# Meta split and row squares put in program order on ScalarE and VectorE, in a hybrid attention layer

## The chip, the core and the metric

The kernel runs on one core of one Trainium2 chip. The time is the device time of one execution in microseconds; lower is better. Each kernel is run several times and the median counts. The engines are named as in the profile: PE is TensorE's matmul, PEld its weight load, DVE VectorE, ACT ScalarE, POOL GpSimd and SP SyncE, whose queue issues nearly all DMAs.

## The reference

One decoder layer over 2048 tokens of width 1024, with 16 learned meta tokens in front. Two kinds of attention run side by side: stick-breaking attention with 8 heads, and a sliding window of 128 with 16 query heads, 2 key heads and a sink per head. Gates merge the two branches, and an RMSNorm ends the layer. Cut to what matters here:

```python
xn = rms_norm(h, norm_gain[l])          # x * rsqrt(mean(x * x) + eps) * gain
proj = xn @ w_in[l]
sb_q, sb_k, sb_v, sw_q, sw_k, sw_v, sb_z, sw_z, g_sb, g_sw = jnp.split(proj, offsets, axis=-1)
# stick-breaking, for each block of 128 queries
mask = (s[None, :] < t[:, None]) & valid[None, :end]
log_beta = jax.nn.log_sigmoid(z)
log_1m = jnp.where(mask, log_beta - z, 0.0)
rev = lax.cumsum(log_1m, axis=3, reverse=True)
suffix = jnp.concatenate([rev[..., 1:], jnp.zeros_like(rev[..., :1])], axis=-1)
w = jnp.where(mask, jnp.exp(log_beta + suffix), 0.0)
o = w @ v
# after both branches
merged = jax.nn.sigmoid(g_sb) * y_sb + jax.nn.sigmoid(g_sw) * y_sw
h = h + merged @ w_out[l]
return rms_norm(h, final_norm_gain)[:, BLOCK:]
```

## The kernel before

The sequence is reversed, so that a running product along a row goes from the newest key to the oldest and ends at the 16 meta columns. The tokens form four groups of 512, handled in two halves: groups 2 and 3 first, then 0 and 1. Each float32 operand of a product is split into a rounded part and the remainder (h and l), and a product is three matmuls: h by h, h by l, l by h.

Each half runs the projections and the window attention (`window`), then the stick-breaking attention (`stick`) with gate projections (`gemm`, L464) woven between its steps. The first half ends with eight pairs of gates that share products (`gate_pairs`); the second goes on to the branch and output projections (`finish`).

The order of work has two sources. PE's instructions run in the order of the program text in the whole kernel. ACT, DVE and SP follow the text only in some stretches (`tc.manual_schedule`). Elsewhere, in `stick` and in `gate_pairs` from its first `ordered()` on, a planner simulates the program when it is built and gives each engine, whenever that is free, the instruction that is then ready and stands first in the text. Each engine then works through its list strictly in order, waiting on the chip wherever an input is late. So an instruction whose inputs are ready early in the simulation is put ahead of work that stands before it in the text.

`stick` walks over steps (h, g, n, j): head, query group, key group counted from the query's, and block of 128 queries.

- `row` makes one row of a step: matmuls into one or two "z" banks (L918), a sigmoid into a row buffer (ACT, L921), in the second half a triangle set to one on POOL (L923), and the running product along the row (DVE, L926 or L928). Where the row ends at the meta columns, POOL copies its last 16 columns to `mr` (L934).
- `turn`, six steps later in the first half and five in the second, transposes four blocks of rows (L943) and splits them with `evac_split`: the copy L126 on ACT, the remainder L127 on DVE.
- `values` multiplies the turned blocks with the values (L975); the last one of a (h, g) copies the sum out (L981) and stores it.
- `split_meta`, called once per (h, g) behind the turn with i = 0 of the last key group, splits `mr` into `m`: the copy L953 on ACT and the remainder L954 on DVE. One turn later, behind the transposes of i = 1, `turn_meta` transposes `m` on PE (L959) and copies the four quarters to `wm` (L963), which a later `values` reads. With 8 heads and 2 groups in each half there are 32 such splits.

`sums_ahead` prepares the norms of the second half's tokens while `gate_pairs` runs. It is advanced once per pair (`next(along, None)`), behind the sigmoid of the pair's first gate (`gate_out`, L1138 or L1141). In each of the first four pairs it loads four tiles of x (128 by 512, into a ring of four buffers, `xs`) and squares them on ACT with a running sum (L1107). With the fifth it makes the reciprocal root (L1112, then `rsqrt`, L131 to L140, with a logarithm and an exponential on ACT). The last pair calls `prep`, which uses the result. A pair's weights are split at L115 and L119, combined at L1078 to L1087, and the combinations split at L1092 and L1094; L1133 adds a product's bank to other sums on DVE and so frees the bank.

Of the kernel before, what the change touches and what calls it, by code (L numbers as in the profile page):

```python
# [10 lines left out]
AF = mybir.ActivationFunctionType  # L11
ALU = mybir.AluOpType
# [31 lines left out]
def f32(ap):  # L44
    return ap.bitcast(F32)
# [3 lines left out]
def tile_kernel(ctx, tc, x, xt, meta, metat, gain, w_in, w_sb, w_sw, w_out, sinks, fgain,  # L49
# [6 lines left out]
    V, A, G, T = nc.vector, nc.scalar, nc.gpsimd, nc.tensor  # L56

    def DMA(dst, src):
        nc.sync.dma_start(*(t.bitcast(F32) if t.dtype == F32R else t for t in (dst, src)))
# [69 lines left out]
    def rsqrt(r, ssq, pool, mid=lambda: None, t=None):  # L129

        V.tensor_scalar(ssq, ssq, 1.0 / D, EPS, op0=ALU.mult, op1=ALU.add)  # L131
        A.activation(r, ssq, AF.Ln)
        A.activation(r, r, AF.Exp, scale=-0.5)
        mid()
        if t is None:
            t = pool.tile([P, 4], F32, tag="nwt", name="nwt", bufs=2)[:r.shape[0], :r.shape[1]]
        V.tensor_tensor(t, r, r, op=ALU.mult)
        V.tensor_tensor(t, t, ssq, op=ALU.mult)
        V.tensor_scalar(t, t, -0.5, 1.5, op0=ALU.mult, op1=ALU.add)
        V.tensor_tensor(r, r, t, op=ALU.mult)  # L140
# [252 lines left out]
    def ring_x(dt=F32):  # L393
        return tp.tile([P, GT], dt, tag="xs", name="xs", bufs=XS)

    def sums():
        return tp.tile([P, 2, 4], F32, tag="ssq", name="ssq", bufs=3)
# [455 lines left out]
    def stick(groups, bp):  # L853
# [96 lines left out]
        def split_meta(h, g):  # L950
            st = state[h, g]
            m = st["m"] = bp.tile([P, 4, 2, NM], F32R, tag="m", name="m", bufs=2)
            A.copy(m[:, :, 0], st["mr"])  # L953
            V.tensor_tensor(m[:, :, 1], st["mr"], f32(m[:, :, 0]), op=ALU.subtract)  # L954

        def turn_meta(h, g):
            p, a = divmod(h, 2)
# [31 lines left out]
        for s in range(n + lt + 3):  # L989
            if s < n:  # L990
                row(*steps[s])
                yield 0.45 if s >= lt else 1.31
            t = s - lt
            if 0 <= t < n:
                turn(*steps[t])
                turned.append(s)
                yield 0.43
                h, g, step, i = steps[t]
                if g + step == 3 and i == 0:
                    split_meta(h, g)  # L1000
                if g + step == 3 and i == 1:
                    turn_meta(h, g)
                    yield 0.11
                if g + step == i == 3:
                    av_todo.append((h, g, vm[:, h // 2, h % 2, :], wm[g % 2], None, False, True))
                    turned.append(s)
            while av_todo and turned[0] < s - 1:
                del turned[0]
                yield values()
# [89 lines left out]
    def sums_ahead(gs_, rs, short):  # L1099

        ssqs = [sums() for _ in gs_]
        todo = [(g, ssq, i, f) for g, ssq in zip(gs_, ssqs) for i in range(4) for f in range(2)]
        while todo:
            for g, ssq, i, f in todo[:4]:
                t = ring_x()
                DMA(t, x[g * GT + i * P:g * GT + (i + 1) * P, f * GT:(f + 1) * GT])
                A.activation(t, t, AF.Square, accum_out=ssq[:, f, i:i + 1])  # L1107
            del todo[:4]
            yield
        t, u = (short()[:, :8] for _ in range(2))  # L1110
        for n, ssq in enumerate(ssqs):
            V.tensor_tensor(t[:, 4 * n:4 * n + 4], ssq[:, 0], ssq[:, 1], op=ALU.add)  # L1112
        rsqrt(rs, t, tp, t=u)
# [237 lines left out]
    for half, groups in enumerate(halves):  # L1351
        gts = [lambda spec=spec: gate(*spec) for spec in specs[half]]
        with tc.tile_pool(name=f"swa{half}", bufs=1, side="left") as sp:
            m = half == 0
# [70 lines left out]
        if half == 0:  # L1425
            with tc.tile_pool(name="fast", bufs=1, side="left") as bp:
                pairs = list(zip(specs[0][-FAST::2], specs[0][-FAST + 1::2]))
                sums_x = combined(*groups, bp, short, *early)
                byhand = ExitStack()
                byhand.enter_context(tc.manual_schedule(engines={mybir.EngineType.DVE}))  # L1430
                with tc.manual_schedule(engines={mybir.EngineType.Activation}):
                    for n in range(PLAIN):
                        w, use, _ = plain[n]
                        for g in groups:
                            next(sums_x[4])
                            if n + 1 == PLAIN and g == groups[1]:
                                drain(first_pair)
                            drain(lagged(col_tile(w, g, use)))
                        if n + 2 < PLAIN:
                            plain.append(gts[rest + n + 2]())  # L1440
                        elif n + 2 == PLAIN:
                            nxt = []
                            first_pair = pair_weights(pairs[0][0][0], pairs[0][1][0], bp, nxt, True)
                            next(first_pair)
                    drain(sums_x[4])
                    sums_x[5]()
                rs = tp.tile([P, 8], F32, tag="rs8", name="rs", bufs=1)
                rs0, rs1 = rs[:, :4], rs[:, 4:]
                gate_pairs(*groups, pairs, bp, sums_x, nxt, byhand.close, sums_ahead(halves[1], rs, short),
                           lambda: prep(halves[1][0], rs0))  # L1450
                hsplit[0] = False
# [68 lines left out]
```

## Time and profile before

| | us |
|---|---|
| median of 3 runs | 2091.56 |
| lowest, highest | 2090.66, 2092.18 |
| profiled execution | 2093.26 |
| its span, first to last instruction | 2091.4 |

The profile is of one execution. Its page gives the busy time of each engine, the span in 40 slices, and the costliest groups of instructions. A timeline row has the start and the duration in us, the engine, the line, the operation, what it writes and reads, and the shape; "x3" stands for three in a row, and the bracket at the end tells how long the engine stood idle before it and what ended that. A row of a tile or a line has the shortest, median and longest duration in ns and the first and last start. Busy times in 40 slices of 52 us each:

```profile
PE   9999999999999999999999999999999999999998
PEld 7888888888888888888888888888888888788887
DVE  7897986877687754887728788777774547464543
ACT  6677774577665335777735555655653212321121
POOL 1233444331000000233310000000000343000000
PEclk9999999999999999999999999999999999999999
```

The first half's stick stage takes slices 8 to 11 (about 360 to 560 us), the gate pairs slices 12 to 15 (about 590 to 745 us), the second half's stick stage slices 22 to 31 (about 1100 to 1590 us). The granted clock is full throughout.

### The profile page before, as it was taken

How to read it: one execution, taken by the hardware profiler on the slowest of the kernel's cores; microseconds unless marked ns; L12 is line 12 of the kernel's file. 1: busy time of each engine (PE TensorE's matmuls, PEld its weight loads, DVE VectorE, ACT ScalarE, POOL GpSimd, SP SyncE). 2: the span in 40 equal slices, each digit the busy share in tenths (PEclk: the TensorE clock that was granted, in tenths of full speed). 3: DMA queues.
4: the chain of work that ended last, by engine and by line, in shares of the span. 5: the costliest groups of instructions: out<-in, count | busy, mean ns of one | idle time of the engine just before them, and what ended most of it. 6: DMA issues, size and time to landing. Idle time of an engine off the chain costs nothing. (4 is left out here: it accounts for less than half of the span.)

```text
span 2091.4 us, 30949 instructions
## 1 busy us (share of the span) xinstructions
PE 2076.3 (99%) x10579; PEld 1744.8 (83%) x10579; DVE 1463.0 (70%) x2383; ACT 1091.4 (52%) x2657; POOL 345.7 (17%) x682
## 2 busy tenths in 40 slices
PE   9999999999999999999999999999999999999998
PEld 7888888888888888888888888888888888788887
DVE  7897986877687754887728788777774547464543
ACT  6677774577665335777735555655653212321121
POOL 1233444331000000233310000000000343000000
PEclk9999999999999999999999999999999999999999
DMA  9855555866377574435455344343424987568532
GB/s 338 307 195 201 188 175 179 252 199 185 91 278 298 209 247 163 159 126 177 150 171 161 120 130 129 114 129 98 121 83 165 350 318 223 182 229 305 154 100 91
DMA packets 170093, 391.46 MB, mean 187 GB/s; under 512 B 23728, under 2 KB 28208, under 8 KB 169936
## 3 DMA queue, kind: packets, MB, share of 16 engines
q1 hardware_dynamic: 169648, 389.23, 55.8%
q8 instruction: 83, 1.36, 0.3%
q14 instruction: 74, 0.61, 0.1%
q10 hardware_dynamic: 288, 0.27, 0.0%
HBM read 241.68 MB, written 145.18 MB: 185 GB/s over the span
## 5 line engine op out<-in xcount | busy, mean ns | idle before, releaser
L464 PE MATMUL ps_g<-xh,wh 128*128 128x512 f32 x1264 | 517.0, 409 | 1.1 <-DVE tmp L680 0.6
L464 PE MATMUL ps_g<-xl,wh 128*128 128x512 f32 x1264 | 495.6, 392 | 0.7 <-DVE xl L1199 0.6
L464 PE MATMUL ps_g<-xh,wl 128*128 128x512 f32 x1264 | 495.7, 392 | 0.0
L928 DVE TENSOR_TENSOR_SCAN row<-row 128x512 f32<-128x512 f32 (+4 forms) x256 | 290.1, 1134 | 116.2 <-POOL row L923 60.1
L464 PEld LDWEIGHTS ps_g<-xh,wl 128*128 128x128 f32 x1264 | 237.8, 188 | 52.7
L464 PEld LDWEIGHTS ps_g<-xh,wh 128*128 128x128 f32 x1264 | 238.5, 189 | 39.9 <-ACT xh L1198 1.4
L464 PEld LDWEIGHTS ps_g<-xl,wh 128*128 128x128 f32 x1264 | 239.2, 189 | 38.0 <-DVE xl L1199 1.8
L921 ACT ACTIVATE row<-ps_z 128x512 f32<-128x512 f32 (+4 forms) x352 | 175.1, 509 | 159.3 <-PE ps_z L918 155.0
L126 ACT ACTIVATE wth<-ps_t 128x512 fp32r<-128x512 f32 (+1 forms) x320 | 171.6, 536 | 61.4 <-PE ps_t L943 59.6
L127 DVE SCALAR_TENSOR_TENSOR wtl<-ps_t,wth 128x512 fp32r<-128x512 f32 (+1 forms) x320 | 188.7, 590 | 21.3 <-ACT wth L126 20.7
L918 PE MATMUL ps_z<-kt,q 128*128 128x512 f32 (+4 forms) x704 | 183.7, 349 | 2.0 <-ACT row L921 1.9
L943 PE MATMUL ps_t<-ident,row 128*128 128x128 f32 x1088 | 171.4, 273 | 1.0 <-DVE wtl L127 0.9
L943 PEld LDWEIGHTS ps_t<-ident,row 128*128 128x128 f32 x1088 | 134.5, 140 | 33.1 <-DVE wtl L127 1.8
L918 PEld LDWEIGHTS ps_z<-kt,q 128*128 128x128 f32 x704 | 124.4, 188 | 27.4 <-ACT row L921 5.1
L975 PE MATMUL ps_o<-wth,vc 128*128 128x512 f32 (+1 forms) x320 | 131.2, 410 | 0.0
L975 PE MATMUL ps_o<-wtl,vc 128*128 128x512 f32 (+1 forms) x320 | 116.4, 364 | 0.0
L767 ACT ACTIVATE sc<-sc,nm 128x129 f32<-128x129 f32 x256 | 100.0, 393 | 30.5 <-DVE nm L765 29.5
L934 POOL COPY mr<-row 128x16 f32<-128x16 f32 x128 | 28.4, 224 | 444.2 <-DVE row L928 401.8
L615 ACT ACTIVATE tmp<-ps_g 128x512 f32<-128x512 f32 x80 | 48.0, 600 | 80.5 <-PE ps_g L464 74.3
L299 ACT CAST ringl<-gt 128x512 fp32r<-128x512 f32 x32 | 19.9, 621 | 127.1 <-DVE gt L297 93.3
L117 POOL TENSOR_SCALAR wh<-raw 128x1024 fp32r<-128x1024 f32 (+1 forms) x45 | 49.8, 1108 | 212.7 <-PE ps_g L464 90.3
L123 POOL TENSOR_TENSOR wl<-raw,wh 128x256 fp32r<-128x256 f32 x88 | 83.2, 975 | 2.0
(442 smaller groups left out, 4202.3 us busy)
## 6 DMA issues: line engine op xcount, KB each, us to landing
wh<-h_in_w_in SPq DMA_DIRECT2D x66, 512.0 KB, 3.9
wl<-l_in_w_in SPq DMA_DIRECT2D x66, 512.0 KB, 5.1
h_in_w_in<-wh SPq DMA_DIRECT2D x50, 512.0 KB, 3.3
l_in_w_in<-wl SPq DMA_DIRECT2D x50, 512.0 KB, 4.1
raw<-in_w_in SPq DMA_DIRECT2D x49, 512.0 KB, 5.3
q<-qd SPq DMA_DIRECT2D x128, 128.0 KB, 3.2
vc<-vd SPq DMA_DIRECT2D x48, 256.0 KB, 3.2
kd<-tmp SPq DMA_DIRECT2D x32, 256.0 KB, 3.4
```

The source lines that it names most:

```text
L117: G.tensor_scalar(h, src, 1.0, 1.0, op0=ALU.mult, op1=ALU.mult)
L123: G.tensor_tensor(l[:, c], src[:, c], f32(h[:, c]), op=ALU.subtract)
L126: A.activation(h, acc, AF.Copy, scale=scale)
L127: V.scalar_tensor_tensor(l, acc, scale, f32(h), op0=ALU.mult, op1=ALU.subtract)
L464: T.matmul(acc, lhsT=a[:, k, :], rhs=b[:, k, :], start=k == i == 0, stop=k == KT - 1 and i == 2)
L615: A.activation(e, acc, AF.Sigmoid)
L767: A.activation(sc[:, hh, :], sc[:, hh, :], AF.Exp, bias=nm[:, hh:hh + 1], accum_out=den[:, hh:hh + 1])
L918: T.matmul(z[:, :m], lhsT=qt[:, j * P:(j + 1) * P], rhs=kt[h][:, k0 + c:k0 + c + m], start=t == 0, stop=t == 1)
L921: A.activation(r[:, c:c + m], z[:, :m], AF.Sigmoid, scale=-1.0)
L928: V.tensor_tensor_scan(r[:, :w], r[:, :w], r[:, :w], last[j] if n else 1.0, op0=ALU.mult, op1=ALU.min)
L943: T.transpose(tr[:, j * P:(j + 1) * P], rows_of[h, g, n - (j > i), j][:, k0:k0 + P], ident)
L975: T.matmul(o[:, :n], lhsT=v, rhs=r, start=first and r is wh, stop=last)
```

## The change

Three instructions change, in two functions. `tc.keep_in_program_order` takes an instruction and orders it, for the planner, behind the instruction that stands before it in the text on the same engine. It adds no wait on the chip, only a place in the engine's list; what stands later in the text may still be planned ahead of it. The change wraps both instructions of `split_meta` and the squares of `sums_ahead` in it. The squares of the first half and every other instruction are as before.

```diff
         def split_meta(h, g):
             st = state[h, g]
             m = st["m"] = bp.tile([P, 4, 2, NM], F32R, tag="m", name="m", bufs=2)
-            A.copy(m[:, :, 0], st["mr"])
-            V.tensor_tensor(m[:, :, 1], st["mr"], f32(m[:, :, 0]), op=ALU.subtract)
+            tc.keep_in_program_order(A.copy(m[:, :, 0], st["mr"]))
+            tc.keep_in_program_order(V.tensor_tensor(m[:, :, 1], st["mr"], f32(m[:, :, 0]), op=ALU.subtract))
...
             for g, ssq, i, f in todo[:4]:
                 t = ring_x()
                 DMA(t, x[g * GT + i * P:g * GT + (i + 1) * P, f * GT:(f + 1) * GT])
-                A.activation(t, t, AF.Square, accum_out=ssq[:, f, i:i + 1])
+                tc.keep_in_program_order(A.activation(t, t, AF.Square, accum_out=ssq[:, f, i:i + 1]))
             del todo[:4]
             yield
```

## The prediction

> **What bounds the kernel now.** I read the page first, then the list of what each engine waited for, then the places that the change touches.
>
> ```profile
> span 2091.4 us, 30949 instructions
> PE 2076.3 (99%) x10579; PEld 1744.8 (83%) x10579; DVE 1463.0 (70%) x2383; ACT 1091.4 (52%) x2657; POOL 345.7 (17%) x682
> ```
>
> TensorE (PE) is busy for 99% of the span, in an order written by hand that the change leaves alone. Time is therefore won or lost only where PE itself starts a matmul later than its stream allows; an idle moment on ScalarE (ACT) or VectorE (DVE) costs nothing by itself. From the list of waits (total us, times, longest us):
>
> ```profile
> PE ps_z L918 <- ACT row L921: 1.9, 3, 1.2
> PE ps_g L1127 <- DVE tmp L1133: 0.6, 1, 0.6
> ...
> ACT m L953 <- POOL mr L934: 10.8, 14, 3.1
> ```
>
> ACT stood 10.8 us in 14 waits in front of the meta copy L953, yet all of PE's waits on the sigmoids that follow it come to 1.9 us. The squares' line tells the same of the other edit:
>
> ```profile
> L1107 ACT ACTIVATE xs<-xs x16: 613/626/634, 599.8 to 631.8; 128x512 f32<-128x512 f32 x16
> ...
>   DMA xs<-in_x: 5.6, 4
> ```
>
> So 16.4 us of standing can go from ACT; what that is worth has to be read on PE.
>
> **The change, part by part.** Each pinned instruction is put behind the one written before it on its engine. Nothing is added or removed: 32 copies (L953), 32 subtractions (L954) and 16 squares move. The meta split's place in the text is right behind the split of the turn with i = 0 (copy L126 on ACT, L127 on DVE). In the trace it runs ahead of that in all 32 cases: the first copy at 380.46 below, its L126 at 382.51. The one reader is the transpose L959:
>
> ```profile
> L953 ACT CAST m<-mr x32: 236/245/247, 380.5 to 1583.7; 128x64 fp32r<-128x64 f32 x32
> L954 DVE TENSOR_TENSOR m<-mr,m x32: 209/221/228, 380.7 to 1584.2; 128x64 fp32r<-128x64 f32 x32
> L959 PE MATMUL ps_o<-ident,m x32: 270/272/273, 383.7 to 1587.6; 128*128 128x128 f32 x32
> ```
>
> *What it gives back.* The 3.1 us wait is the first copy's (ACT's timeline, then PE's):
>
> ```profile
> 380.46 0.24 ACT L953 CAST m<-mr 128x64 fp32r<-128x64 f32 x1 [3.13 <-POOL mr L934]
> 380.61 1.08 ACT L921 ACTIVATE row<-ps_z 128x512 f32<-128x512 f32 x2
> 382.02 0.60 ACT L921 ACTIVATE row<-ps_z 128x512 f32<-128x512 f32 x1 [0.33 <-PE ps_z L918]
> 382.51 0.59 ACT L126 ACTIVATE wth<-ps_t 128x512 fp32r<-128x512 f32 x1
> ...
> 379.40 0.39 PE L464 MATMUL ps_g<-xl,wh 128*128 128x512 f32 x1
> 379.63 0.39 PE L464 MATMUL ps_g<-xh,wl 128*128 128x512 f32 x1
> 381.25 0.50 PE L918 MATMUL ps_z<-kt,q 128*128 128x512 f32 x1 [1.24 <-ACT row L921]
> ```
>
> Two sigmoids (L921) stand behind the copy, and PE waits for the bank that the first of them frees: from 379.63 to 381.25 are 1.62 us from start to start, where 0.23 is usual (379.40 to 379.63). Gain 1.39 us. PE's two other waits on L921 also have a copy ahead of the sigmoid:
>
> ```profile
> 486.08 0.24 ACT L953 CAST m<-mr 128x64 fp32r<-128x64 f32 x1 [0.28 <-POOL mr L934]
> 486.66 0.63 PE L918 MATMUL ps_z<-kt,q 128*128 128x400 f32 x2 [0.18 <-ACT row L921]
> ...
> 508.60 0.24 ACT L953 CAST m<-mr 128x64 fp32r<-128x64 f32 x1
> 510.21 0.63 PE L918 MATMUL ps_z<-kt,q 128*128 128x400 f32 x2 [0.52 <-ACT row L921]
> ```
>
> A wait hides some 0.16 us more in the matmul before it (1.39 against the 1.24 shown). So PE lost 0.34 us at 486, all of which the copy and its wait can explain, and 0.68 at 508, of which the copy alone is 0.24 at most; I take half of that, since work on ACT overlaps. The meta split gives back 1.85 us.
>
> *What it costs.* The split now comes late for L959. Typical places of the two halves' stages, and the tightest:
>
> ```profile
> 397.23 0.69 DVE L127 SCALAR_TENSOR_TENSOR wtl<-ps_t,wth 128x512 fp32r<-128x512 f32 x1 [0.42 <-ACT wth L126]
> 397.83 0.14 PEld L959 LDWEIGHTS ps_o<-ident,m 128*128 128x128 f32 x1
> 397.84 0.97 DVE L926 TENSOR_TENSOR_SCAN row<-row,mask 128x144 f32<-128x144 f32 x1
> 397.94 0.27 PE L959 MATMUL ps_o<-ident,m 128*128 128x128 f32 x1
> ...
> 1247.64 0.67 DVE L127 SCALAR_TENSOR_TENSOR wtl<-ps_t,wth 128x512 fp32r<-128x512 f32 x1
> 1248.42 0.27 PE L959 MATMUL ps_o<-ident,m 128*128 128x128 f32 x1
> 1248.55 1.23 DVE L928 TENSOR_TENSOR_SCAN row<-row 128x512 f32<-128x512 f32 x1 [0.25 <-POOL row L923]
> ...
> 538.27 0.66 DVE L127 SCALAR_TENSOR_TENSOR wtl<-ps_t,wth 128x512 fp32r<-128x512 f32 x1
> 538.29 0.27 PE L959 MATMUL ps_o<-ident,m 128*128 128x128 f32 x1
> ```
>
> A DVE instruction can start 0.61 us behind L127 (397.23 to 397.84), L954 lasts 0.22, PE follows a releaser by 0.04 (the first of the two sigmoids, 0.60 like the single one, ends at 381.21, PE goes on at 381.25), and the weight load leads its matmul by 0.11 (397.83 to 397.94). So L959 can start 0.98 us behind L127. Now it starts 0.71 behind at 397, 0.78 at 1247 and 0.02 at 538; it will be late by 0.27, 0.20 and 0.96 us, and PE stands as long, for its queue is in order: behind L959 stand value matmuls, the next rows and the woven gate matmuls. I made this subtraction at all 32 places. In the first half's stage nine of 15 come out short, by 3.7 us together; the first place, whose DVE is late through the wait that goes, I count at their mean, 0.25. In the second half's stage 13 of 16 are short, by 2.2 us. Cost 6.1 us. The 0.98 is a sum of four rows, not seen as a whole; each tenth of a microsecond in it is 2.2 us here, so 3.9 to 8.3 us for a tenth either way.
>
> The rest of the move lies beside other work. The copy fits on ACT, idle for half of the time, between L126 and the next sigmoid. L954 fits in the second half's stage between L127's end at 1248.31 and the scan at 1248.55; in the first half's it pushes the scan by its 0.22 us, and the scan's row is turned only six steps later. Without that cover these 16 pushes would cost 3.5 us. The wm copies L963 move with L959, and their reader comes two turns later. POOL's buffers of mr are held some 2 us longer at the first place, and there are two of them.
>
> The rows let a DVE instruction start at 397.84, before L127 ends at 397.92. The Trainium skill ("VectorE: DVE Perf Modes", section "The DRAIN you can't avoid") says that the next one does not start until the pipe is empty; by that L954 would start at 0.69 and the sum be 1.8 us higher. The trace disagrees with it for this pair of instructions.
>
> *The squares.* All 16 are now pulled ahead to 599.8 to 632 us; pinned, they come in fours behind the first sigmoid of gate pairs 0 to 3. (Last row: us and instructions busy in a stretch on PE, PEld, DVE, ACT, POOL, then clock, DMA share, GB/s.)
>
> ```profile
> 603.58 0.63 ACT L1107 ACTIVATE xs<-xs 128x512 f32<-128x512 f32 x1 [3.01 <-DMA xs<-in_x]
> 607.89 1.90 DVE L1094 TENSOR_TENSOR sl<-tmp,sh 128x512 fp32r<-128x512 f32 x3 [1.60 <-ACT sh L1092]
> 609.50 0.39 PE L1129 MATMUL ps_t<-xh,wl 128*128 128x512 f32 x1
> 610.53 0.47 PE L1127 MATMUL ps_g<-t2h,sh 128*128 128x512 f32 x1 [0.64 <-DVE tmp L1133]
> ...
> 601.54 5.63 SPq L59 DMA_DIRECT2D xs<-in_x  x4
> 637.05 1.28 ACT L133 ACT_TABLE_LOAD   x1
> 655.00 0.63 ACT L1138 ACTIVATE tmp<-tmp 128x512 f32<-128x512 f32 x1
> ...
> 655.00:670.00 15.00, 15.00 (x68) 12.43 (x67) 11.53 (x18) 6.30 (x10) 0.00 (x0) 1.00 0.55 207
> ```
>
> Squares that wait for their x hold ACT, so the weight copies L1092 come late, DVE waits 1.60 us for them, its add L1133 frees the bank late, and PE stands: 610.53 - 609.50 - 0.23 = 0.80 us. That is the gain; it is nothing if another late copy takes the place. The 16 loads of x move too, since their four buffers come free later. SyncE's queue (SP) stood 5.63 us over four such loads, with gate stores and weight loads behind it. A load queued ahead of its square could hold the next pair's weights as long; against that ACT has room: in the pair at 655 it is busy for 6.30 of 15 us, and four squares (2.5 us at 0.63) with the three table loads around the logarithm and the exponential (3.8 us at 1.28), which now fall there, fit into the 8.7 us left. I take 0, with the two bounds 5.6 us of loss and no gain beyond the 0.80.
>
> *Sum*: -1.85 + 6.1 - 0.80 = +3.45 us. The profiled execution took 2093.26 us (its span 2091.4 and 1.9 around it); the sum makes that 2096.7. It lay 1.7 us above the median of 2091.56, so the median becomes 2095.0 us, my forecast.
>
> **The rivals.** *The scan gets in between.* The planner, not the text, decides what DVE runs behind L127. Where the next scan goes first, L954 waits for one more scan, 0.97 to 1.23 us in the rows above, and nearly every L959 is late by it: about 1.06 us more over the first stage's 16 places makes +17, 2112; over both stages +34, 2129. For it: in the first stage the scan follows L127 without a gap, so it is ready. Against: L954 stands ahead of that scan in the text, and DVE keeps scan, split, scan in the order of the text around all these places. It decides from the point where a scan is ready before the copy L953 has ended; in a few places alone it makes 2098 to 2104. Chance 0.20.
>
> *L959 does not stand* (DVE, freed of the early L954, runs its L127 sooner): only the gain of 2.65 us stays, 2088.9. For it: at 538 L127 runs late behind other DVE work, which can fall otherwise. Against: 22 short places are too many for chance. Chance 0.18.
>
> *Faster by more.* The waits of PE that the moved instructions can reach are the 1.9 and 0.6 us above and 0.16 us hidden behind each of the four, 3.1 us; 2088.4 is the floor of the edits, and below it other orders of the planner would have to improve. Chance 0.12.
>
> *L954 waits for the end of L127* (0.69 instead of 0.61, at 22 places): +5.25, 2096.8; the scan at 397.84 speaks against it. Chance 0.05. *The pins move nothing*: excluded by the copies that now run ahead of their L126; 2091.6, chance 0.02.
>
> **How the numbers follow.** My forecast has 0.43, with 2092 to 2098 as its own range. A measurement of this kernel tells 0.2%, 4.2 us, from no change: under 2087.4 is faster, over 2095.7 slower. The forecast's centre is 0.7 us inside, so 0.27 of it goes to the same and 0.16 to slower. The scan rival (0.20) and the pipe (0.05) are slower; of the second rival 0.15 is the same and 0.03 faster; 0.12 is faster and 0.02 the same. Slower 0.41, same 0.44, faster 0.15. The range's low end, 2087.5, takes in the case without stalls; the high end, 2103, takes in some scans in between and leaves out the full rival.
>
> **What would show it.** Right: ACT's wait at L953 for POOL gone, PE's wait for row L921 at 380 gone, new waits of PE at L959 on DVE m L954, 0.1 to 0.9 us each; groups of four squares behind the first sigmoid of four pairs, and no PE wait at 610. Wrong: a scan between L127 and L954 (the first rival); no waits at L959 (the second); a change of PE's waits outside the two stages and the pairs, which would mean that other orders of the planner decided.

## The result, and the profile after

| | us |
|---|---|
| before, median of 22 runs | 2091.07 (2089.27 to 2093.00) |
| after, median of 22 runs | 2094.28 (2093.16 to 2096.64) |
| profiled execution after | 2093.48, span 2091.6 |

The change makes the kernel slower by 3.2 us: the ratio is 1.0015, with a 95% interval of 1.0009 to 1.0021. That is clear of no change. It lies in the forecast's own range of 2092 to 2098, 0.7 us below its centre of 2095.0.

The spans of the two profiles differ by only 0.2 us (2091.4 and 2091.6), so they cannot simply be subtracted. PE runs the same list of 10579 matmuls in both kernels, so each matmul's start can be compared with its own start before. Summed over stretches (us from the start of the span before; after minus before), that gives

```
stretch         0-16   16-369  369-562  562-600  600-620  620-1095  1095-1600  1600-2080
after          -2.35    +0.27    +2.56    +0.01    -1.20     +0.01      +1.43      -0.42
```

The first 16 us are the start of the kernel, which no edit touches. The profiled execution of before was slow there: all eight kernels below are 1.5 to 2.2 us shorter in that stretch too, and that is about what the profile before lay above its median. What is left is the first half's stick stage (+2.56), the start of the gate pairs (-1.20) and the second half's stick stage (+1.43): +2.8 us, against 3.2 measured by the medians.

The page and the list of waits of the changed kernel (us in total, times, longest us):

```profile
span 2091.6 us, 30928 instructions
PE 2076.0 (99%) x10579; PEld 1742.2 (83%) x10579; DVE 1459.2 (70%) x2383; ACT 1089.9 (52%) x2657; POOL 347.5 (17%) x682
...
PE ps_o L959 <- DVE m L954: 3.3, 6, 1.7
PE ps_z L918 <- ACT row L921: 0.4, 1, 0.4
```

The busy times say nothing, as before. The waits do: PE's wait for L921 fell from 1.9 to 0.4 us, and a wait that was not there, of the transpose L959 for the subtraction L954, leads PE's list. Three of these transposes with what stands ahead of them:

```profile
1247.32 0.67 DVE L127 SCALAR_TENSOR_TENSOR wtl<-ps_t,wth 128x512 fp32r<-128x512 f32 x1
1247.90 0.21 DVE L954 TENSOR_TENSOR m<-mr,m 128x64 fp32r<-128x64 f32 x1
1248.17 0.14 PEld L959 LDWEIGHTS ps_o<-ident,m 128*128 128x128 f32 x1 [0.33 <-DVE m L954]
1248.17 0.33 PE L959 MATMUL ps_o<-ident,m 128*128 128x128 f32 x1
1248.25 0.48 PE L975 MATMUL ps_o<-wth,vc 128*128 128x512 f32 x1
...
395.25 0.69 DVE L127 SCALAR_TENSOR_TENSOR wtl<-ps_t,wth 128x512 fp32r<-128x512 f32 x1 [0.41 <-ACT wth L126]
395.79 2.25 POOL L123 TENSOR_TENSOR wl<-raw,wh 128x256 fp32r<-128x256 f32 x3
395.86 0.73 DVE L954 TENSOR_TENSOR m<-mr,m 128x64 fp32r<-128x64 f32 x1
396.64 0.14 PEld L959 LDWEIGHTS ps_o<-ident,m 128*128 128x128 f32 x1 [0.76 <-DVE m L954]
396.64 0.33 PE L959 MATMUL ps_o<-ident,m 128*128 128x128 f32 x1 [0.53 <-DMA kt<-kd]
...
372.83 8.48 DVE L926 TENSOR_TENSOR_SCAN row<-row,mask 128x528 f32<-128x528 f32 x7
377.59 3.71 POOL L934 COPY mr<-row 128x16 f32<-128x16 f32 x4
381.33 0.24 ACT L953 CAST m<-mr 128x64 fp32r<-128x64 f32 x1 [1.14 <-POOL mr L934]
381.23 0.66 DVE L127 SCALAR_TENSOR_TENSOR wtl<-ps_t,wth 128x512 fp32r<-128x512 f32 x1
381.81 0.21 DVE L954 TENSOR_TENSOR m<-mr,m 128x64 fp32r<-128x64 f32 x1
382.08 0.33 PE L959 MATMUL ps_o<-ident,m 128*128 128x128 f32 x1 [1.73 <-DVE m L954]
```

At 1247 L954 follows L127 at once, and L959 starts 0.06 us after L954 ends. The weight load and the matmul of the transpose now start together, and the matmul lasts 0.33 us where it lasted 0.27. At 395 the same, but L954 takes 0.73 us; the DMA in the bracket of the matmul is not what PE stood for, since the weight load of the same transpose waits for L954 until the same moment. The last group is the first place of all. ACT's wait shrank from 3.13 to 1.14 us, but PE stands 1.73 us at L959, because DVE works through seven scans before it comes to L127. POOL's copies hold the place nearly as long: the copy L953 behind them ends at 381.57, 0.24 us before L954 starts.

The squares' line, and the pinned squares of the first pair:

```profile
L1107 ACT ACTIVATE xs<-xs x16: 614/616/629, 604.9 to 656.1; 128x512 f32<-128x512 f32 x16
...
604.39 0.63 ACT L1141 ACTIVATE tmp<-tmp 128x512 f32<-128x512 f32 x1 [4.25 <-DVE tmp L1133]
604.93 0.62 ACT L1107 ACTIVATE xs<-xs 128x512 f32<-128x512 f32 x1
606.77 1.13 ACT L1092 CAST sh<-tmp 128x512 fp32r<-128x512 f32 x2
657.82 1.28 ACT L132 ACT_TABLE_LOAD   x1
```

They reach to 656 instead of 632 us and wait for no load any more (the 5.6 us before are gone), the weight copies L1092 run between them, and no PE wait is left in the pairs. The table loads moved from 635 to 658 us, and PE has no wait there.

### The profile page after: what moved, and what is told of

Its sections match the earlier page's. It is cut to its first block, busy times and chain, and to the rows that moved or that the text cites. A ratio compares the mean times of both kernels' runs of the same rounds, so it can differ in the third digit from the quotient of the medians.

```text
span 2091.6 us, 30928 instructions
## 1 busy us (share of the span) xinstructions
PE 2076.0 (99%) x10579; PEld 1742.2 (83%) x10579; DVE 1459.2 (70%) x2383; ACT 1089.9 (52%) x2657; POOL 347.5 (17%) x682
## 4 chain that ended last, share of the span: by engine, by line
PE 90%; DVE 4%; ACT 2%; DMA 1%; issue 1%; SPq 0%; POOL 0%; DVEq 0%; ACTq 0%; POOLq 0%
PE ps_g L464 38%; PE ps_o L975 6%; PE ps_z L918 6%; PE ps_t L943 5%; PE ps_z L759 3%; PE ps_o L815 2%; PE ps_g L260 1%; PE ps_g L259 1%; PE ps_g L258 1%; PE ps_t L793 1%; PE ps_z L260 1%; PE ps_z L259 1%; PE ps_z L258 1%; PE ps_t L260 1%; PE ps_t L259 1%; PE ps_t L258 1%
## 5 line engine op out<-in xcount | busy, mean ns | idle before, releaser
L921 ACT ACTIVATE row<-ps_z 128x512 f32<-128x512 f32 (+4 forms) x352 | 175.0, 508 | 165.3 <-PE ps_z L918 161.4
L127 DVE SCALAR_TENSOR_TENSOR wtl<-ps_t,wth 128x512 fp32r<-128x512 f32 (+1 forms) x320 | 188.6, 590 | 25.1 <-ACT wth L126 24.5
L934 POOL COPY mr<-row 128x16 f32<-128x16 f32 x128 | 30.3, 238 | 445.6 <-DVE row L928 403.3
L117 POOL TENSOR_SCALAR wh<-raw 128x1024 fp32r<-128x1024 f32 (+1 forms) x45 | 52.1, 1158 | 212.1 <-PE ps_g L464 50.3
L926 DVE TENSOR_TENSOR_SCAN row<-row,mask 128x512 f32<-128x512 f32 (+2 forms) x64 | 69.6, 1095 | 22.5 <-ACT row L921 21.8
```

Of the source, the lines that this page charges most:

```text
L127: V.scalar_tensor_tensor(l, acc, scale, f32(h), op0=ALU.mult, op1=ALU.subtract)
L921: A.activation(r[:, c:c + m], z[:, :m], AF.Sigmoid, scale=-1.0)
L926: V.tensor_tensor_scan(r[:, :w], r[:, :w], mask[:, :w], 1.0, op0=ALU.mult, op1=ALU.max)
```

## The experiments

Two accounts stood against each other. The first is that of the forecast: PE stands at L959 for the late split, and gets back the waits that the early copies and squares had caused. The second: other orders that the planner chose after the change make the time.

The traces limit the second account from the start. With only the meta split pinned (e1 below), every other instruction on PE, ACT, DVE and POOL runs in the order of before. In the full change ACT and DVE have another order beyond the moved instructions only between 608 and 661 us, in the gate pairs. In the stick stages nothing but the splits moved.

Stretches as above, for all kernels in the order of the experiments below (us against the profile before; the columns 562-600 and 620-1095 are within 0.4 us everywhere; where L959 is moved, PE's list differs around its places only). From 1600 us to the end all are within 1 us but e5, whose profiled execution is 2.66 us longer there, where nothing was edited; its median does not show it.

```
                  369-562  600-620  1095-1600   median us (before beside it)
after               +2.56    -1.20      +1.43   2094.28 (2091.07)
e1_meta_only        +2.71    -0.39      +1.39   2094.97 (2091.06)
e2_squares_only     -0.01    -1.20      +0.01   2090.06 (2091.06)
e3_turn_late        -1.92    -1.20      -0.01   2089.37 (2091.06)
e4_split_early      -0.68    -1.20      -0.02   2090.01 (2091.06)
e5_late_no_pins     -0.27    -0.85      +0.05   2090.38 (2090.77)
e7_dve_only         +4.63    -1.20      +1.51   2096.51 (2090.77)
e8_first_later      -2.64    -1.20      +0.05   2087.93 (2090.77)
e9_first_four       +0.00    -1.20      +0.01   2090.84 (2090.77)
```

**The meta split alone.**

```diff
-            A.copy(m[:, :, 0], st["mr"])
-            V.tensor_tensor(m[:, :, 1], st["mr"], f32(m[:, :, 0]), op=ALU.subtract)
+            tc.keep_in_program_order(A.copy(m[:, :, 0], st["mr"]))
+            tc.keep_in_program_order(V.tensor_tensor(m[:, :, 1], st["mr"], f32(m[:, :, 0]), op=ALU.subtract))
```

> Only the two instructions of split_meta are pinned; the squares are as before. Theory (PE stands at L959 behind the late split, and the squares give back a wait of their own): the two stick stages lose 2.6 and 1.4 us as in the trace after, the gate pairs are as before with their PE wait at 610 us: about 2095.1, +4.0 us (+0.19%). Rival (other orders of the planner, which differ in many lists after the change, make the difference): nothing fixed, near the changed kernel's +3.2 or anywhere between 0 and +3.

2094.97 us, ratio 1.0021 (1.0012 to 1.0029). Both stick stages repeat those of the full change to 0.15 us, so the squares have no part in them, and the same wait leads PE's list:

```profile
PE ps_o L959 <- DVE m L954: 3.3, 6, 1.7
```

Pinning the copy alone is no case of its own: the planner then makes the same list on every engine as with both pinned.

**The squares alone.**

```diff
-                A.activation(t, t, AF.Square, accum_out=ssq[:, f, i:i + 1])
+                tc.keep_in_program_order(A.activation(t, t, AF.Square, accum_out=ssq[:, f, i:i + 1]))
```

> Only the squares are pinned; split_meta is as before. Theory: no PE wait at L959, the wait for POOL at 380 us is there, the PE waits at 610 and 613 us are gone: 2089.9, -1.2 us (-0.06%). Rival (the pinned squares only trade one wait for another, and the gain in the trace came from the shifted stick stage before): within 0.3 us of the kernel before, with a PE wait of 0.5 us or more in the gate pairs.

2090.06 us, ratio 0.9998 (0.9989 to 1.0007): the time does not tell it from no change. The trace does: PE loses nothing in the pairs, 1.20 us less from 600 to 620 us, and both stick stages are as before to a hundredth. The wait list has the old rows again and none at L959:

```profile
PE ps_z L918 <- ACT row L921: 1.9, 3, 1.2
PE ps_o L90 <- POOL mx L87: 1.3, 1, 1.3
PE ps_t L943 <- DVE wtl L127: 0.9, 2, 0.6
```

But the 1.20 us belong to the one execution profiled. Other kernels that leave the squares unpinned were also 0.39, 0.85 and 1.20 us shorter than before in this stretch (e1, e5, e7). So the wait that the pin removes cost 1.20, 0.81, 0.35 and 0 us in four executions, 0.6 in the mean. In these four the first weight copy L1092 starts 7.0, 6.7, 6.2 and 5.6 us behind the same matmul of PE, that at 600 us before: the longer the squares hold it, the longer PE stands. In all six profiled executions with pinned squares the wait is gone. The medians fit: the full change lies 0.7 us below the meta split alone.

**The change with the transpose one turn later.**

```diff
-                if g + step == 3 and i == 1:
+                if g + step == 3 and i == 2:
                     turn_meta(h, g)
```

> The changed kernel, with turn_meta (the transpose L959 and the copies L963) one turn later, behind i = 2. Theory: L959 now comes some 2 us later in PE's list, so the split is there in time at all places but perhaps the first; the 5.2 us of standing at the other 31 go, and the gains stay: 2087 to 2088.5. Rival (the standing at L959 is not what costs, PE would wait at the next place anyway): 2093.5 or more, with new PE waits behind L943 or L918 in its place.

2089.37 us, 4.9 us less than the full change (ratio to before 0.9993, 0.9984 to 1.0001). No wait at L959 is left, and the second stick stage is back at its old length. In the first one wait of the first place stays: there the copy L953 still waits for POOL, and PE behind it.

```profile
382.61 0.64 PE L918 MATMUL ps_z<-kt,q 128*128 128x272 f32 x3 [1.68 <-ACT row L921]
383.99 0.27 PE L959 MATMUL ps_o<-ident,m 128*128 128x128 f32 x1
```

The standing at L959 was thus the cost, and it does not come back at the next place. The time is 0.9 us above the expected 2087 to 2088.5.

**The change with the split one turn earlier.** PE's list stays as it is.

```diff
-                if g + step == 3 and i == 0:
-                    split_meta(h, g)
+                for k in [0] * (t == 0 and g == 3) + [t + 1] * (t + 1 < n and sum(steps[t + 1][1:3]) == 3 and steps[t + 1][3] == 0):
+                    split_meta(*steps[k][:2])
```

> The changed kernel, with the call of split_meta one turn earlier in the text (the first one of each half's first head stays where a turn before it is lacking), both still pinned. PE's list is the same as in both kernels. Theory: the split is done some 2 us before L959, no standing there but at the first place of the first half (1.9 us), and the copy comes late enough not to wait for POOL long: 2088 to 2090. Rival (pinned at all, the copy or the subtraction holds ACT or DVE and costs as much elsewhere): 2093 or more.

2090.01 us, ratio 0.9994 (0.9985 to 1.0003), in the range expected. Of PE's waits at L959 the one of the first place is left, whose split could not be moved:

```profile
PE ps_o L959 <- DVE m L954: 1.7, 1, 1.7
```

It is not the pin that costs, but that the place in the text is one turn too close to the reader.

**The later transpose without any pin.** The edit of the third experiment on the kernel before.

> The kernel before, without any pin, with turn_meta one turn later (behind i = 2). Theory: there is no standing at L959 before the change, so a later L959 has nothing to give: stick stages within 0.3 us of before, 2091 us. Rival (the later transpose is better by itself, and the gain of the changed kernel with the late turn over the changed kernel is that): 2 us or more faster than before.

2090.38 us, ratio 1.0000 (0.9990 to 1.0009); stick stages -0.27 and +0.05 us. The later transpose has nothing to give where the split is early.

**The subtraction alone.**

```diff
-            V.tensor_tensor(m[:, :, 1], st["mr"], f32(m[:, :, 0]), op=ALU.subtract)
+            tc.keep_in_program_order(V.tensor_tensor(m[:, :, 1], st["mr"], f32(m[:, :, 0]), op=ALU.subtract))
```

> Only the subtraction L954 is pinned (VectorE); the copy L953 runs ahead as before, the squares are as before. Theory: what PE stands for at L959 is VectorE's place, so the second half's stage loses the same 1.4 us, and the first half's loses the 3.9 us of its 15 places, while the copy's waits at 380, 486 and 508 us stay and nothing is given back: first stage +3.5 to +4.5, together +5 to +6 us, 2096 to 2097. Rival (the copy's place on ScalarE is the late one): L959 does not wait, within 1 us of before.

2096.51 us, ratio 1.0026 (1.0015 to 1.0037): slower than the full change, and in the range expected (the first stage is 0.1 us above its own). The costs are all there, and the waits behind the copy at 381, 486 and 508 us are not given back. The first place shows both waits, one behind the other:

```profile
379.54 0.24 ACT L953 CAST m<-mr 128x64 fp32r<-128x64 f32 x1 [3.13 <-POOL mr L934]
...
380.33 0.73 PE L918 MATMUL ps_z<-kt,q 128*128 128x512 f32 x2 [1.22 <-ACT row L921]
384.54 0.33 PE L959 MATMUL ps_o<-ident,m 128*128 128x128 f32 x1 [1.54 <-DVE m L954]
```

**The later transpose, and at the first place split and transpose another turn later.**

```diff
-                if g + step == 3 and i == 0:
+                if g + step == 3 and i == (t < 4 and g == 3):
                     split_meta(h, g)
-                if g + step == 3 and i == 1:
+                if g + step == 3 and i == 2 + (t < 4 and g == 3):
                     turn_meta(h, g)
```

> The changed kernel with turn_meta one turn later, and at the very first (head, group) of the first half, where mr comes late, the split one turn later and the transpose two turns later. Theory: the wait of 1.7 us that PE keeps at the first place with the late turn alone goes, since the split then stands behind the turn with i = 1, when POOL's copies are done: first stage 3 to 3.5 us shorter than before, the gate pairs 1.2, together 2086.5 to 2087.5. Rival (the backlog of seven scans on VectorE at the start of the stage holds PE there whatever the split's place): no faster than the late turn alone, 2089.

2087.93 us, ratio 0.9987 (0.9979 to 0.9996): faster than both kernels, 0.4 us above the expected range (the first stage gives 2.64 us, not 3 to 3.5). The first place's wait is down to 0.27 us, and no row of L959 is left:

```profile
381.61 0.63 PE L918 MATMUL ps_z<-kt,q 128*128 128x272 f32 x3 [0.27 <-ACT row L921]
384.73 0.27 PE L959 MATMUL ps_o<-ident,m 128*128 128x128 f32 x1
```

This version keeps what the change was able to give back (2.64 us in the first stick stage) and pays next to nothing.

**Only the first four squares pinned.**

```diff
-                A.activation(t, t, AF.Square, accum_out=ssq[:, f, i:i + 1])
+                (tc.keep_in_program_order if i < 2 and g == gs_[0] else (lambda ins: ins))(A.activation(t, t, AF.Square, accum_out=ssq[:, f, i:i + 1]))
```

> Of all changes only the first four squares are pinned; the twelve others and split_meta are as before. Theory: the PE waits at 610 and 613 us come from the squares that stand ahead of the weight copies while their x is under way, and those are the first four: the stretch from 600 to 620 us is 1.2 us shorter, as with all 16 pinned. Rival (it is the spreading of all 16 loads and squares over four pairs that relieves the queue): 0.4 us or less, with a PE wait left at 610.

2090.84 us, ratio 0.9999 (0.9990 to 1.0009). In the trace the stretch from 600 to 620 us is 1.20 us shorter, with twelve squares still pulled ahead:

```profile
L1107 ACT ACTIVATE xs<-xs x16: 614/617/632, 602.6 to 629.5; 128x512 f32<-128x512 f32 x16
```

That fits the first four, but it does not settle it: in the execution of the subtraction alone the wait was absent with no square pinned. Whether spreading the other twelve adds anything stays open.

## Why the prediction was right, point by point

**PE stands at L959.** Right in kind and place. L954 follows L127 with no scan in between at all 32 places, as the forecast assumed; the first rival did not come. In the first half's 15 later places PE's starts slip by 3.85 us (3.7 forecast), in the second half's 16 by 1.35 us (2.2 forecast). At 429 us the start slips by only 0.07 us, where 0.40 was forecast, and L127 itself came 0.26 us sooner against PE's matmuls: at that one place some of the second rival came true. A sign of being right failed: ACT's wait at L953 for POOL was to be gone, and 1.14 us of it stayed.

**The 0.98 us between L127 and L959 was too long.** The term that was off is the 0.11 us for the weight load ahead of its matmul. When PE has waited, both start together, and L959 starts 0.85 us behind L127 (1247.32 to 1248.17). Of that only 0.06 us return as a longer matmul (0.33 against 0.27): 0.91 us in effect. In the second stage, where nearly all places were short by 0.1 to 0.2 us, 13 times 0.07 us are the whole difference. In the first stage it was made up for by something not foreseen, two subtractions that took 0.73 and 0.81 us instead of 0.22.

**The first place.** Here a step failed: the forecast took 1.39 us back and charged a mean 0.25 us. The old wait did go, and so did one of 0.29 us at the next turn (which goes with the subtraction alone pinned too, so it is not part of the old one). But the text's place put the split behind an L127 that stands behind seven scans, and PE lost 1.95 us at L959. Net loss 0.3 us where a gain of 1.1 us was forecast. I had called that lateness a result of the removed stall; it is DVE's own backlog at the start of the stage, with POOL's copies, slow beside those scans, hardly sooner.

**The other returns.** 0.35 us at 486 us as forecast, 0.15 at 508 us for 0.12. A wait of 0.44 us at 457 us went that the forecast had left out; some 0.6 us more lie in steps of under 0.15 us, whose causes stay open. With them the first stage came to +2.56 us where the forecast's terms made +2.1.

**The squares.** 1.20 us in the profiled execution for 0.80 forecast (the small gap behind it was 0.2 and another 0.2 lay around). The bound of 5.6 us for SyncE's queue was not needed: at 612 us ACT stood 2.16 us for weights, where it stood 1.44 before, but PE had no wait in the pairs. The table loads found room on ACT. Over the four executions above the wait is worth about 0.6 us, since it comes and goes with the moment at which the squares let the weight copies through. Stick stages and 0.6 us make 2.56 + 1.43 - 0.6 = +3.4 us, against +3.2 measured and +3.45 forecast. That the sum is so close is luck, since the errors of its terms cancel: the first place cost 1.4 us more, the second stage 0.85 less, and unlisted waits gave 1.0 back.

**The rivals.** Other orders of the planner left no mark: in the stick stages there are none, and outside the three stretches the kernels agree with the profile before within 0.9 us in each stretch from 16 to 1600 us. L954 started 0.58 us behind L127 (1247.32 to 1247.90), before L127 ended at 1247.99, and 0.58 to 0.61 us behind it at all 32 places, so it did not wait for the end of the one before. The prediction took that for a contradiction of the Trainium skill ("VectorE: DVE Perf Modes", section "The DRAIN you can't avoid"). It need not be one: the same section adds that a next instruction which is not held starts earlier.

## What to carry to other kernels

An instruction that a planner pulls ahead shows as idle time on its own engine; price that at what the bounding engine waits behind it (here 2 of 10.8 us), not at its length. Tying it to its place in the text is safe only if the text gives its reader as much lead as the planner did, so check the reader's start against the earliest end at the new place, at every occurrence and above all at the first, where queues are still filling. Here moving the reader by one turn took away the loss of 3.2 us, and moving split and reader by another turn at the first place made it a gain of 2.8 us. Where two kernels share the bounding engine's list, comparing the starts of its instructions one by one shows tenths of a microsecond that the total time hides.

## What the runs showed of the hardware

**POOL and DVE shut each other out.** A meta copy L934 of 128 by 16 takes 0.20 us on POOL when it is alone. After the change four of them took 3.71 us at the first place while DVE ran scans without a pause (the rows at 372.83 and 377.59 above): three took 1.17 us each, about the length of a scan (1.19). Before the change DVE paused from 380.04 us on, for the split, and the same four took 0.76 us:

```profile
379.67 0.76 POOL L934 COPY mr<-row 128x16 f32<-128x16 f32 x4
```

In the traces before and after, nine copies started in the middle of a scan, and each ended 8 to 10 ns before that scan did. The three of 1.17 us started in the last 0.07 us of one scan and ended 7 to 8 ns before the next one did; one that started so with no scan behind took its 0.19 us. It goes the other way too: the subtraction L954, 0.21 us else, took 0.73 us beside POOL's L123 at 395.79, and 0.81 beside L117:

```profile
450.72 1.04 POOL L117 TENSOR_SCALAR wh<-raw 128x1024 fp32r<-128x1024 f32 x1 [6.99 <-PE ps_g L464]
...
450.45 0.66 DVE L127 SCALAR_TENSOR_TENSOR wtl<-ps_t,wth 128x512 fp32r<-128x512 f32 x1
451.03 0.81 DVE L954 TENSOR_TENSOR m<-mr,m 128x64 fp32r<-128x64 f32 x1
```

The scan and the subtraction both read two tensors from SBUF; L127, which reads one of its two from PSUM, ran its usual 0.66 us beside the same L117, and 134 copies that ran beside L127 alone took 0.19 to 0.20 us. The Trainium skill says as much ("SBUF — State Buffer", section "Who interferes with whom"): a DVE instruction with two SBUF inputs contends with a GpSimd instruction that reads SBUF, and the pair of ports that the two engines share is an exclusive lock. The traces agree, with 1.17 for 0.20 us on the one side and 0.73 for 0.21 on the other. A 0.2 us copy can so become the last thing that ACT waits for, here 1.14 us at 381.33.
